# W_v in column quarters, five x buffers, a halved norm scaling, and a list scheduler that counts table loads, in an eight-core encoder block

## The chip, the cores and the metric

The kernel runs on the eight cores of one Trainium2 chip. Every core computes one of eight batch entries with the same program; the cores exchange nothing. The metric is device microseconds of the slowest core. A run on eight cores can be in a slower state: one die, or both, is granted a lower TensorE clock and the run takes some per cent longer. Stage times are medians over the eight cores of one profiled fast run. Ratios are the mean time of one kernel's fast runs over that of the other's fast runs of the same rounds, so they are not quite the ratio of the medians quoted. "The V stage ends" means the start of its last matmul; in the same way attention ends with its last product with V, the convolution with the first matmul on W_out, and the output projection with the last one.

## The reference, cut to what matters

```python
# x (8, 2048, 2048) f32; one layer
h = rms_norm(x, ln1_g)
u = h @ W_in                                # 2048 -> 5120: conv value, conv gate, q, k, v
y_conv = conv_mixer(c_val, c_gate, ...)     # GLU, causal depthwise conv (31), LayerNorm, swish
y_attn = chunked_relbias_attention(q, k, v) # 8 heads of 128, 64-frame chunks, 9-chunk band
y = concat(rms_norm(y_conv), rms_norm(y_attn))
x = x + y @ W_out
x = x + relu(rms_norm(x) @ W1)**2 @ W2      # 2048 -> 8192 -> 2048
```

On a core the program has five stages: norm and V projection ("V stage"), attention with the q and k projections, convolution, output projection (beside the convolution group's normalisation), and feed-forward.

## The kernel before

The program is a list of operations. When the kernel is built, a list scheduler places them with a simple cost model and thereby fixes the order on each engine; at run time each engine works through its list and waits on semaphores. An operation at the head of a list that has to wait therefore blocks everything behind it, ready or not. The dependencies come from a table of who last wrote or read each granule of 64 bytes in SBUF:

```python
XLAT = 180.0
DMA_LAT = 2000.0
DMA_BPNS = 310.0          # the scheduler's belief of the DMA rate, bytes per ns
...
    # Prog.keys: an access touches these granules of SBUF
    for g in range(a // 64, (e - 1) // 64 + 1):
        for q in range(p0 // 32, (p0 + np_ - 1) // 32 + 1):
            out.add(g * 4 + q)
...
    # Prog.schedule: the ready operation of lowest program number goes next
            o.start = c
            busy[e] = c + o.dur
            if o.dma:
                s = max(dma_free, busy[e])
                dma_free = s + o.bytes / DMA_BPNS     # one first-in-first-out pipe
                o.end = dma_free + DMA_LAT
...
                rt[s] = max(rt[s], o.end + lat)       # when a successor may start
```

The V stage. A tile of x is normalised into `hb`, transposed on TensorE, copied to `hT`, and multiplied by W_v into a bank of PSUM, the memory that matmuls write to. The eviction is the ScalarE operation that copies the result from the bank to V. V has a row of 8 heads x 130 elements for every tile of 128 tokens (two further columns of ones give the softmax sums):

```python
V = sb("V", [16, 8, 130], BF16, B)
wv = sb("wv", [2, 16, 512], BF16, C)                   # W_v in two column halves
xs1 = [sb(f"xa{i}", [2048], F32, D0 + 8192 * i) for i in range(3)]
...
loadx(0); pv; gr                                       # gr: the norm's gain row
for j in range(4):                                     # gain row to all partitions
    mm(ps(4 + j), <ones>, gr[0:1, j * 512:(j + 1) * 512], True, True)
    copy(g1[:, j * 512:(j + 1) * 512], ps(4 + j))      # VectorE
for q in range(4):                                     # first half, in quarters of its rows
    P.dma("pool", f"wv0{q}", wv[:, 0, 4 * q:4 * q + 4, :], ...)
late = [... second half, after tile 1 ...]

def norm_tile(xt, t, st, r, g, hbuf, dst, banks):
    act(hbuf[:, :], xt, AF.Square, accum=st[:, t, 0:1])
    act(st[:, t, 1:2], st[:, t, 0:1], AF.Ln, ...)
    act(r[:, t:t + 1], st[:, t, 1:2], AF.Exp, scale=-0.5)
    stt(hbuf[:, :], xt, r[:, t:t + 1], g, ALU.mult, ALU.mult)    # the scaling
    ... 16 transposes on TensorE, two copies to hT ...

for t in range(NT):
    norm_tile(...)
    for hf in range(2):
        b = nb[0] % 4                                  # four PSUM banks in turn
        nb[0] += 1
        for k in range(16):
            mm(ps(b), hT[...tile t, block k...], wv[:, hf, k, :], k == 0, k == 15)
        act(V[:, t, 4 * hf:4 * hf + 4, 0:128], ps(b)..., AF.Identity)   # the eviction
```

`norm_tile` also serves the second norm (tile h2b), inside the output projection stage.

## Time and profile before

Four timed runs took 2789.91, 2790.71, 2901.05 and 3006.79 us, the last two slow; the profiled run took 2791.73 us and is a fast one.

From the profile page of the kernel before (its slowest core): the span, TensorE's busy time, TensorE's busy tenths in 40 slices, and the granted clock in tenths.

```profile
span 2790.2 us, 37523 instructions; the slowest of 8 cores (2783.8 to 2790.2 us)
PE 2727.9 (98%) x14192; PEld 1271.9 (46%) x14192; DVE 930.0 (33%) x1460; ACT 822.6 (29%) x1561; POOL 227.9 (8%) x367
PE   6999999999989999999999999999999999999999
PEclk9999999999999999999999999999999999999999
```

TensorE is the bound, and 98% busy looks like nothing is left. But a busy TensorE need not be at its peak. Taking from the timeline the time from each matmul's start to the next one's, and subtracting its columns at 2.4 GHz, leaves about 117 us (core 3; 2654 us are the columns). Two places stand out: the first 60 us (23 us of it) and 700 to 1020 us (39 us). Another 34 us lie in small pieces between 100 and 700 us.

The windows view of core 3 before, in stretches of 100 us (stretch, its length, busy us and instruction count of TensorE, weight loads, VectorE, ScalarE, GpSimd; then the granted clock, DMA share and GB/s):

```profile
700.00:800.00 100.00, 88.36 (x640) 42.46 (x639) 82.79 (x110) 60.85 (x86) 22.73 (x22) 1.00 0.54 148
800.00:900.00 100.00, 90.18 (x532) 44.48 (x531) 66.75 (x93) 63.18 (x82) 1.79 (x2) 0.97 0.46 132
900.00:1000.00 100.00, 96.00 (x551) 47.91 (x550) 51.12 (x58) 38.84 (x54) 1.43 (x2) 0.98 0.47 143
1300.00:1400.00 100.00, 100.00 (x465) 45.37 (x464) 17.87 (x26) 19.66 (x32) 5.71 (x8) 1.00 0.46 75
```

The last line is the feed-forward part: 465 matmuls of 512 columns in 100 us, 215 ns each, with no gap. In the three lines above it TensorE sits idle part of the time. The waits view of core 3 before (who waited for whom: total us, times, longest) names the largest:

```profile
PE ps L158 <- DVE h2b L193: 13.8, 4, 4.1
PE ps L158 <- DVE hb_75 L193: 8.9, 3, 4.3
PE ps L158 <- DVE hb_76 L193: 5.1, 2, 3.4
```

h2b is the second norm's scaled tile, in the output projection; hb is the first norm's, in the V stage. The start is best read in the timeline of TensorE on core 3 before (start, length, operation, count, and in brackets the idle time before it and what ended that):

```profile
6.63 7.16 PE L154 MATMUL ps<-gr,onef 1*128 1x512 f32 x8 [6.63 <-DMA gr<-gvec]
17.37 1.86 PE L158 MATMUL ps<-identb,hb_75 128*128 128x128 bf16 x16 [3.58 <-DVE hb_75 L193]
19.44 1.86 PE L154 MATMUL ps<-wv,hT 128*128 128x512 bf16 x4 [0.20 <-DVE hT L184]
...
30.86 11.21 PE L154 MATMUL ps<-wv,hT 128*128 128x512 bf16 x40
...
50.30 7.99 PE L154 MATMUL ps<-wv,hT 128*128 128x512 bf16 x32
```

By 50 us only 48 V matmuls of 512 columns are done; from then on TensorE does not stop. The V stage ends at 161.5 us.

One more view matters, the ScalarE timeline before (core 5), in the output projection:

```profile
812.61 0.61 ACT L173 ACTIVATE jk_122<-sl_120 128x512 bf16<-128x512 f32 x1
813.23 1.28 ACT L173 ACT_TABLE_LOAD   x1
814.52 0.30 ACT L173 ACTIVATE st<-st,pv 128x1 f32<-128x1 f32 x1
```

A change between Silu and Ln or Exp costs a table load of 1.28 us. The profile has 25 of them, and the scheduler's model has none.

### The profile page before, as it was taken

What the parts mean: (1) busy time and instruction counts of PE and PEld (TensorE: products, weight loads), DVE (VectorE), ACT (ScalarE), POOL (GpSimd) and SP (SyncE); (2) the same over time, 40 slices, a digit from 0 to 9 for tenths busy, and PEclk for the clock granted to TensorE, in tenths of its full rate; (3) what the DMA queues carried; (4) which work ended last, traced back from release to release, by engine and by line L of the source; (5) the groups of instructions that cost most, each with busy time, mean ns of one, the idle gap of its engine ahead of it and who ended that gap; (6) DMA issues with size and microseconds to landing.
All of it is one profiled execution on the core that took longest, in us unless ns stands there. A gap on an engine that the chain in (4) does not pass through costs nothing.

```text
span 2790.2 us, 37523 instructions; the slowest of 8 cores (2783.8 to 2790.2 us)
## 1 busy us (share of the span) xinstructions
PE 2727.9 (98%) x14192; PEld 1271.9 (46%) x14192; DVE 930.0 (33%) x1460; ACT 822.6 (29%) x1561; POOL 227.9 (8%) x367
## 2 busy tenths in 40 slices
PE   6999999999989999999999999999999999999999
PEld 3545555444444444444444444444444444444444
DVE  3435556555876532021131120221311302203113
ACT  3437777211485331201202112112021021120220
POOL 0000000423300000000000000000000000000000
PEclk9999999999999999999999999999999999999999
DMA  8611110335644467444444444468644444444424
GB/s 197 153 33 35 35 28 2 61 55 88 146 137 136 136 151 183 79 76 78 80 76 77 78 76 76 76 137 195 136 76 76 76 76 76 77 77 76 78 41 136
DMA packets 112737, 256.77 MB, mean 92 GB/s; under 512 B 5425, under 2 KB 83249, under 8 KB 95153
## 3 DMA queue, kind: packets, MB, share of 16 engines
q0 software_dynamic: 92400, 167.82, 36.8%
q1 hardware_dynamic: 20162, 86.56, 8.9%
q8 instruction: 117, 1.92, 0.3%
q14 instruction: 58, 0.48, 0.1%
HBM read 388.60 MB, written 33.55 MB: 151 GB/s over the span
## 4 chain that ended last, share of the span: by engine, by line
PE 93%; DVE 2%; ACT 2%; issue 2%; DMA 1%; POOL 0%; SPq 0%; DVEq 0%; ACTq 0%; POOLq 0%
PE ps L154 91%; PE ps L158 1%; DMA xa_73<-x 1%; DVE Gt_110 L201 0%; DVE h2b L193 0%; DMA eB_94<-relb 0%; DVE Gt_109 L201 0%; DVE G L193 0%; ACT L173 0%; DVE y L193 0%; DVE y L201 0%; DVE hb_75 L193 0%; POOL pad L184 0%; ACT cs L173 0%; ACT hb_75 L173 0%
## 5 line engine op out<-in xcount | busy, mean ns | idle before, releaser
L187 DVE TENSOR_TENSOR acc<-acc,ps 128x512 f32<-128x512 f32 x512 | 351.7, 688 | 1412.3 <-PE ps L154 1408.5
L154 PE MATMUL ps<-yb,fT 128*128 128x512 bf16 x2752 | 598.8, 379 | 0.0
L154 PEld LDWEIGHTS ps<-yb,fT 128*128 128x128 bf16 x2752 | 269.0, 98 | 325.1 <-issue 1.6
L173 ACT ACTIVATE rl_131<-ps 128x512 f32<-128x512 f32 x128 | 76.6, 598 | 1101.1 <-PE ps L154 1098.5
L154 PE MATMUL ps<-w2s_135,fT 128*128 128x512 bf16 x1344 | 293.9, 379 | 0.0
L154 PE MATMUL ps<-hTb,yb 128*128 128x512 bf16 x1024 | 242.1, 379 | 0.0
L154 PE MATMUL ps<-yb 128*128 128x512 bf16 x1024 | 241.9, 379 | 0.0
L154 PEld LDWEIGHTS ps<-w2s_135,fT 128*128 128x128 bf16 x1344 | 131.5, 98 | 158.6 <-issue 0.3
L220 POOL DMA_DIRECT2D yb<-w x75 | 66.3, 883 | 1189.4 <-PE ps L154 1112.4
L173 ACT ACTIVATE rl_132<-ps 128x512 f32<-128x512 f32 x128 | 76.6, 598 | 270.8 <-PE ps L154 270.8
L154 PEld LDWEIGHTS ps<-yb 128*128 128x128 bf16 x1024 | 100.2, 98 | 120.8
L154 PEld LDWEIGHTS ps<-hTb,yb 128*128 128x128 bf16 x1024 | 100.1, 98 | 120.6
L154 PE MATMUL ps<-yb,w1s_133 128*128 128x512 bf16 x512 | 121.0, 379 | 0.0
L154 PE MATMUL ps<-hTb,w1s_134 128*128 128x512 bf16 x512 | 121.0, 379 | 0.0
L154 PE MATMUL ps<-yb,w1s_134 128*128 128x512 bf16 x512 | 121.0, 379 | 0.0
L154 PE MATMUL ps<-hTb,w1s_133 128*128 128x512 bf16 x512 | 120.9, 379 | 0.0
L154 PE MATMUL ps<-wo,yT 128*128 128x512 bf16 x512 | 119.0, 386 | 1.4 <-ACT yT L173 0.9
L154 PE MATMUL ps<-hT,wc_101 128*128 128x512 bf16 x512 | 119.6, 379 | 0.0
L154 PE MATMUL ps<-wo,yb 128*128 128x512 bf16 x512 | 118.5, 389 | 0.0
L154 PE MATMUL ps<-wv,hT 128*128 128x512 bf16 x512 | 116.5, 389 | 0.4 <-DVE hT L184 0.2
L154 PE MATMUL ps<-hT,wc_102 128*128 128x512 bf16 x512 | 116.1, 379 | 0.9 <-DMA wc_102<-wcg 0.9
L154 PE MATMUL ps<-hT,wqk_66 128*128 128x512 bf16 x384 | 97.1, 379 | 0.0
(269 smaller groups left out, 2688.8 us busy)
## 6 DMA issues: line engine op xcount, KB each, us to landing
yb<-w POOLq DMA_DIRECT2D x75, 1024.0 KB, 8.8
w2s_135<-w POOLq DMA_DIRECT2D x21, 1024.0 KB, 8.4
w1s_133<-w POOLq DMA_DIRECT2D x16, 1024.0 KB, 8.4
w1s_134<-w POOLq DMA_DIRECT2D x16, 1024.0 KB, 8.4
acc<-out SPq DMA_DIRECT2D x16, 1024.0 KB, 9.8
out<-acc SPq DMA_DIRECT2D x64, 256.0 KB, 5.8
wo<-wo POOLq DMA_DIRECT2D x8, 1024.0 KB, 13.7
xa_71<-x SPq DMA_DIRECT2D x6, 1024.0 KB, 6.7
```

What stands on the lines that cost most here:

```text
L154: self.op("pe", lambda e: e.matmul(out, lhsT=lhsT, rhs=rhs, start=start, stop=stop, skip_group_check=skip), [lhsT, rhs], [out], f * max(n ...
L158: self.op("pe", lambda e: e.transpose(out, in_, ident), [in_, ident], [out], 64.0)
L173: self.op("act", lambda e: e.activation(out=out, in_=in_, func=func, scale=scale, bias=bias, **kw), r, w, d)
L187: self._ew(eng, lambda e: e.tensor_tensor(out=out, in0=in0, in1=in1, op=op), [in0, in1], [out], fast)
L220: o = self.op(eng, lambda e: e.dma_start(out=out, in_=in_), r, w, 900.0 if eng == "pool" else 350.0, dma=True, key=key, nbytes=nb)
```

## The change

Its intent: feed TensorE earlier at the start, and give the scheduler a truer model, so that the fixed order blocks less. The diff cut to its core:

```diff
+SLACK = 400.0
+TABLE = 1300.0
+    SETS = ((AF.Exp, AF.Ln), (AF.Exp, AF.Tanh), (AF.Silu,))
             busy[e] = c + o.dur
+            if o.func in (AF.Exp, AF.Ln, AF.Tanh, AF.Silu) and o.func not in tset:
+                tset = next(s for s in self.SETS if o.func in s)
+                busy[e] += TABLE
...
+                if so.eng == "pe" and e != "pe":
+                    lat += SLACK          # TensorE may use another engine's result 400 ns later
...
-    wv = sb("wv", [2, 16, 512], BF16, C)
+    wv = sb("wv", [4, 16, 256], BF16, C)
-    xs1 = [... for i in range(3)]
+    xs1 = [... for i in range(5)]         # and hb from two buffers to three
-    loadx(0); pv; gr
+    gr; loadx(0); identity; pv            # the gain row first
-        copy(g1[...], ps(4 + j))
+        copy(...) if j % 2 else act(..., AF.Identity)
+    ld = []
+    for j in range(4):
+        ld.append(P.dma("pool", f"wv{j}", wv[:, j, :, :], wv_d[j]))
+        if j == 0:
+            for t in range(1, 5):
+                loadx(t)
...
-        stt(hbuf[:, :], xt, r[:, t:t + 1], g, ALU.mult, ALU.mult)
+        for hf in range(2):
+            c = slice(1024 * hf, 1024 * hf + 1024)
+            stt(hbuf[:, c], xt[:, c], r[:, t:t + 1], g[:, c], ALU.mult, ALU.mult)
...
+            if hf and t < 8: act(o_, src, AF.Identity)   # every other hT copy of the first 8 tiles
...
-        for hf in range(2):
-            b = nb[0] % 4
+        for hf in range(4):                              # bank = quarter
             for k in range(16):
-                mm(ps(b), hT[...], wv[:, hf, k, :], k == 0, k == 15)
-            act(V[:, t, 4 * hf:4 * hf + 4, 0:128], ...)
+                mm(ps(hf, 0, 256), hT[...], wv[:, hf, k, :], k == 0, k == 15)
+            act(V[:, t, 2 * hf:2 * hf + 2, 0:128], ...)
+    for j in (1, 2, 3):
+        ld[j].deps.add(xo_[2 * j - 1].i)                 # quarters 2, 3, 4 after x tiles 1, 3, 5
```

Smaller edits are cut: the modelled byte count of a DMA now uses its true number of partitions, and the hT copies are modelled as faster.

More of the change, by code (lines that the diff above doesn't have):

```diff
@@ L28 @@
 class Op:
-    __slots__ = ("i", "eng", "fn", "dur", "deps", "dma", "key", "cnt", "bytes", "prio",
+    __slots__ = ("i", "func", "eng", "fn", "dur", "deps", "dma", "key", "cnt", "bytes", "prio",
                  "start", "end", "pos", "signal", "waits", "ins")
@@ L44, in __init__ @@
         self.cnt = 0
+        self.func = None
 class Prog:
@@ L172, in act @@
             d += 100
-        self.op("act", lambda e: e.activation(out=out, in_=in_, func=func, scale=scale, bias=bias, **kw), r, w, d)
+        self.op("act", lambda e: e.activation(out=out, in_=in_, func=func, scale=scale, bias=bias, **kw), r, w, d).func = func
     def _ew(self, eng, fn, r, w, fast=1.0):
@@ L181, in _ew, with copy @@
         self.op(eng, fn, r, w, d)
-    def copy(self, out, in_, eng="dve"):
-        self._ew(eng, lambda e: e.tensor_copy(out=out, in_=in_), [in_], [out])
+    def copy(self, out, in_, eng="dve", fast=1.0):
+        self._ew(eng, lambda e: e.tensor_copy(out=out, in_=in_), [in_], [out], fast)
     def tt(self, out, in0, in1, op, eng="dve", fast=1.0):
@@ L218, in dma @@
                 l.append(x)
-                nb = max(nb, self.n(x) * 128 * 4)
+                nb = max(nb, self.n(x) * x.ap[0][1] * 4)
         o = self.op(eng, lambda e: e.dma_start(out=out, in_=in_), r, w, 900.0 if eng == "pool" else 350.0, dma=True, key=key, nbytes=nb)
@@ L240, in schedule @@
         dma_free = 0.0
+        tset = ()
         for o in ops:
@@ L394, in build_program @@
     x_d = dr("x", [S, D])
-    wv_d = dr("wv", [2, 128, 16, 512])
+    wv_d = dr("wv", [4, 128, 16, 256])
     wqk_d = dr("wqk", [8, 2, 128, 16, 128])
@@ L471, in build_program @@
     wqk = [sb(f"wqk{i}", [16, 128], BF16, o + 16384 + 4096 * i) for i in range(3)]
-    wv = sb("wv", [2, 16, 512], BF16, C)
+    wv = sb("wv", [4, 16, 256], BF16, C)
     on = sb("on", [16, 1024], BF16, C)
-    xs1 = [sb(f"xa{i}", [2048], F32, D0 + 8192 * i) for i in range(3)]
+    xs1 = [sb(f"xa{i}", [2048], F32, (D0, D0 + 8192, D0 + 16384, B + 33280, B + 41472)[i]) for i in range(5)]
     g1 = sb("g1", [2048], F32, D0 + 24 * KB)
-    hb = [sb(f"hb{i}", [2048], BF16, D0 + 32 * KB + 4096 * i) for i in range(2)]
+    hb = [sb(f"hb{i}", [2048], BF16, (D0 + 32 * KB, D0 + 36 * KB, B + 57856)[i]) for i in range(3)]
+    xo_ = {}
     def loadx(t):
-        P.dma("sp", f"xa{t % 3}", xs1[t % 3][:, :], x_d[t * 128:(t + 1) * 128, :])
+        xo_[t] = P.dma("sp", f"xa{t % 5}", xs1[t % 5][:, :], x_d[t * 128:(t + 1) * 128, :])
     def bcast(g, n):
         return bass.AP(gv_d.tensor, g * 2048, [[0, 128], [1, n]])
-    loadx(0)
-    P.dma("sp", "pv", pv[:, :], pv_d)
     gr = sb("gr", [2048], F32, D0 + 42 * KB)
     P.dma("sp", "gr", gr[0:1, :], gv_d[0:1, :])
+    loadx(0)
+    P.dma("pool", "id", identb[:, :], id_d)
+    P.dma("sp", "pv", pv[:, :], pv_d)
     P.memset(onef[:, :], 1.0, "dve")
@@ L491, in build_program @@
         mm(ps(4 + j), bass.AP(onef, 0, [[1, 1], [0, 128]]), gr[0:1, j * 512:(j + 1) * 512], True, True)
-        copy(g1[:, j * 512:(j + 1) * 512], ps(4 + j))
-    P.dma("pool", "id", identb[:, :], id_d)
-    P.dma("sp", "sel", sel[:, :], id_d[:, 0:4])
-    for q in range(4):
-        P.dma("pool", f"wv0{q}", wv[:, 0, 4 * q:4 * q + 4, :], wv_d[0][:, 4 * q:4 * q + 4, :])
-    late = [P.dma("pool", f"wv1{q}", wv[:, 1, 8 * q:8 * q + 8, :], wv_d[1][:, 8 * q:8 * q + 8, :]) for q in range(2)]
-    loadx(1)
-    loadx(2)
+        if j % 2:
+            copy(g1[:, j * 512:(j + 1) * 512], ps(4 + j))
+        else:
+            act(g1[:, j * 512:(j + 1) * 512], ps(4 + j), AF.Identity)
+    ld = []
[4 more added lines that the diff above has]
+                loadx(t)
+            P.dma("sp", "sel", sel[:, :], id_d[:, 0:4])
     P.ts(pv[:, bdw2:bdw2 + 8], pv[:, bdw:bdw + 8], 2.0, ALU.mult)
@@ L506, in build_program @@
     P.memset(V[:, :, :, 128:130], 1.0, "pool")
-    nb = [0]
     def norm_tile(xt, t, st, r, g, hbuf, dst, banks):
-        act(hbuf[:, :], xt, AF.Square, accum=st[:, t, 0:1])
+        act(hbuf[:, :], xt[:, :], AF.Square, accum=st[:, t, 0:1])
         act(st[:, t, 1:2], st[:, t, 0:1], AF.Ln, scale=1.0 / D, bias=pc(epsc))
         act(r[:, t:t + 1], st[:, t, 1:2], AF.Exp, scale=-0.5)
-        stt(hbuf[:, :], xt, r[:, t:t + 1], g, ALU.mult, ALU.mult)
+        for hf in range(2):
+            c = slice(1024 * hf, 1024 * hf + 1024)
+            stt(hbuf[:, c], xt[:, c], r[:, t:t + 1], g[:, c], ALU.mult, ALU.mult)
         for hf in range(2):
@@ L527, in dst @@
             o_ = hT[:, qd, 8 * hf:8 * hf + 8, ti * 128:(ti + 1) * 128]
-            copy(o_, src)
-        norm_tile(xs1[t % 3][:, :], t, st, rn, g1[:, :], hb[t % 2], dst, (4 + 2 * (t % 2), 5 + 2 * (t % 2)))
-        if t + 3 < NT:
-            loadx(t + 3)
-        if t == 1:
-            for o_ in late:
-                o_.deps.add(len(P.ops) - 1)
+            if hf and t < 8:
+                act(o_, src, AF.Identity)
+            else:
+                copy(o_, src, fast=1.9)
+        norm_tile(xs1[t % 5], t, st, rn, g1, hb[t % 3], dst, (4 + 2 * (t % 2), 5 + 2 * (t % 2)))
+        if t + 5 < NT:
+            loadx(t + 5)
         if t == 8:
             mark = len(P.ops) - 1
-        for hf in range(2):
-            b = nb[0] % 4
-            nb[0] += 1
+        for hf in range(4):
             for k in range(16):
-                mm(ps(b), hT[:, qd, k, ti * 128:(ti + 1) * 128], wv[:, hf, k, :], k == 0, k == 15)
-            act(V[:, t, 4 * hf:4 * hf + 4, 0:128], ps(b).rearrange("p (h c) -> p h c", c=128), AF.Identity)
+                mm(ps(hf, 0, 256), hT[:, qd, k, ti * 128:(ti + 1) * 128], wv[:, hf, k, :], k == 0, k == 15)
+            act(V[:, t, 2 * hf:2 * hf + 2, 0:128], ps(hf, 0, 256).rearrange("p (h c) -> p h c", c=128), AF.Identity)
+    for j in (1, 2, 3):
+        ld[j].deps.add(xo_[2 * j - 1].i)
     q32 = [sb(f"q32{i}", [512], F32, D0 + 40 * KB + 2048 * i) for i in range(2)]
@@ L800, in out_conv @@
         P.dma("sp", f"xw{t % 3}", out_d[t * 128:(t + 1) * 128, :], xs[t % 3][:, :], w=[("x1", t)])
-        norm_tile(xs[t % 3][:, :], t, st, rn, g2[:, :], h2b, dst, (3, 4))
+        norm_tile(xs[t % 3], t, st, rn, g2, h2b, dst, (3, 4))
     conv_load(0)
@@ L965, in _prep_shared @@
     wvv = win[:, 4096:5120]
-    wv = np.stack([kc(wvv[:, i * 512:(i + 1) * 512], 512) for i in range(2)])
+    wv = np.stack([kc(wvv[:, i * 256:(i + 1) * 256], 256) for i in range(4)])
     wcg = np.stack([np.stack([kc(win[:, o + i * 128:o + (i + 1) * 128], 128) for o in (0, 1024)], 1) for i in range(8)])
```

## The prediction

> All numbers are of the fast state (profiled run 2791.73 us; the timed runs of 2901 and 3007 us are read as slow ones). A slow run would lie some per cent above.
>
> **What bounds it now.** TensorE: 98% busy on the page, 91% of the chain of waits. Charging every matmul of the timeline its columns at 2.4 GHz gives about 2654 us; start-to-start time beyond that is about 121 us, plus 8.0 us before the first matmul. From 1020 us on (feed-forward) the windows view shows 465 matmuls per 100 us, 215 ns each: the change can't touch it. The excess lies in three places: 0 to 60 us, about 30 us with the 8 us before the first matmul; 100 to 700 us (attention, convolution), about 34 us in small pieces; 700 to 1000 us (output projection beside the convolution group's normalisation), about 40 us.
>
> **The start.** Before, the gain row lands at 7.96 us, its broadcast takes 7.16 us, four VectorE copies end at 15.9, the scaling takes 2.35, and the first transpose starts at 18.70. Four matmuls on W_v run at 20.8; the rest of its first half waits until 32.9 us (timeline); the second half, issued at 35.2, comes around 50. By 50.9 us TensorE has done about 15 us of work. DMA is 90 to 100% busy until 60 us, so only order helps. After: the gain row lands near 4 us, the copies alternate with ScalarE, the scaling comes in halves (about 1.2 us each): first transpose near 13 us. Four x tiles and one column quarter at a time give complete accumulations earlier: estimated 30 us of useful work by 50 us. Saved: 16 us (8 to 22). Added: V is 1024 matmuls of 256 columns instead of 512 of 512, about 3 ns more each (2 us), and 32 more evictions on ScalarE, 40 to 50% busy there.
>
> **The scheduler.** The trace has 25 table loads of 1283 ns, 21 of them in 700 to 1000 us, which the old cost model counted as nothing. The Trainium skill ("ScalarE: Activation LUTs", What ACT_TABLE_LOAD costs) gives about 1283 ns plus a drain; the trace agrees on the load. The static TensorE order therefore reaches transposes too early: four waits for h2b, 13.9 us in all (waits view). Such waits also drop the clock: the windows view shows 0.95 to 0.98 in 700 to 1000 us, about 10 us; the skill ("TensorE: Matmul & The Clock Gate", What's actually happening) describes this half rate after idling, and this trace has such stretches of 3.4 us. I expect the table cost, the 400 ns slack and the first scaling half to take away 18 us here (8 to 26), and the slack about 6 us (0 to 12) in 100 to 700 us. Table loads themselves: still 20 to 30.
>
> **Sum.** 2791.7 - 16 - 18 - 6 = about 2752 us, -1.4%. Range 2725 to 2785. Over 2% needs 56 us of roughly 130 removable at most: 0.2. Slower by 2%: 0.02. Within 2%: 0.78.
>
> **What would show it.** First transpose at 12 to 14 us; end of the V stage (162.8 us before) at 143 to 152; waits for h2b below 5 us; clock in 700 to 900 us above 0.98; feed-forward still 215 ns per matmul, starting about 40 us earlier.
>
> **What would make it wrong.** The x tiles sharing DMA with the first column quarter so that it lands after 25 us, and later quarters waiting behind x: the start gains little. A static order that puts V of a late quarter ahead of transposes and blocks. Slack pulling filler work forward, so that the stage from 700 us lacks it. New stalls in the feed-forward part. And a gain near 50 us if the waits of 700 to 1000 us vanish wholly.

## The result, and the profile after

Four fast runs took 2782.34 to 2785.23 us, median 2783.81. The fast runs' ratio to those of the kernel before is 0.9977, 95% interval 0.9953 to 1.0001: the same, where 0.986 was forecast. From the profile page after (the profiler lost some matmul records of this core):

```profile
span 2782.1 us, 38484 instructions; the slowest of 8 cores (2778.2 to 2782.1 us)
PE 2707.2 (97%) x14445; PEld 1327.1 (48%) x14704; DVE 932.3 (34%) x1482; ACT 830.9 (30%) x1601; POOL 228.1 (8%) x365
PE   4999999999989999999999999999999999999999
PEclk8999999999999999999999999999999999999999
```

The first slice fell from 6 to 4 tenths, and its clock from 9 to 8: the start got worse. The other end of the argument went as forecast. The windows view of core 3 after:

```profile
700.00:800.00 100.00, 89.61 (x676) 43.26 (x673) 76.97 (x100) 53.53 (x76) 30.84 (x29) 0.95 0.57 142
800.00:900.00 100.00, 97.74 (x575) 47.85 (x576) 79.12 (x115) 67.26 (x91) 2.00 (x2) 0.97 0.49 148
900.00:1000.00 100.00, 100.00 (x600) 50.22 (x599) 56.31 (x69) 43.07 (x56) 1.92 (x3) 1.00 0.47 148
1300.00:1400.00 100.00, 100.00 (x465) 45.31 (x463) 17.73 (x27) 19.62 (x32) 5.18 (x7) 1.00 0.47 79
```

TensorE is busy for 97.74 and 100 us where it was for 90.18 and 96, and the feed-forward line is unchanged. The waits of core 3 after: those for hb doubled, from 14.0 to 28.4 us, and h2b almost went.

```profile
PE ps L163 <- DVE hb_77 L198: 11.5, 5, 4.1
PE ps L163 <- DVE hb_78 L198: 9.7, 6, 3.4
PE ps L163 <- DVE hb_79 L198: 7.2, 1, 7.2
...
PE ps L163 <- DVE h2b L198: 1.1, 2, 0.6
```

The start on TensorE, core 3 after:

```profile
2.92 7.16 PE L159 MATMUL ps<-gr,onef 1*128 1x512 f32 x8 [2.92 <-DMA gr<-gvec]
14.15 2.10 PE L163 MATMUL ps<-identb,hb_77 128*128 128x128 bf16 x16 [4.07 <-DVE hb_77 L198]
21.10 3.57 PE L159 MATMUL ps<-wv,hT 128*128 128x256 bf16 x16 [4.84 <-DMA wv<-wv]
...
29.22 1.91 PE L159 MATMUL ps<-wv,hT 128*128 128x256 bf16 x8
...
31.57 1.07 PE L159 MATMUL ps<-wv,hT 128*128 128x256 bf16 x8
...
41.09 1.01 PE L163 MATMUL ps<-identb,hb_78 128*128 128x128 bf16 x8 [3.35 <-DVE hb_78 L198]
...
50.52 1.01 PE L163 MATMUL ps<-identb,hb_79 128*128 128x128 bf16 x8 [7.22 <-DVE hb_79 L198]
51.33 3.62 PE L159 MATMUL ps<-wv,hT 128*128 128x256 bf16 x16
```

The transposes do start earlier (17.4 to 14.2 us). The first weight quarter is there at 21.0. But between 32.6 and 51.3 us there is no V matmul at all, only transposes waiting for later x tiles; by 50.5 us 32 V matmuls of 256 columns are done, a third of the work that was done before. In that stretch the data are there: the trace has the second quarter landing at 38.0 us, the third at 46.7, and four tiles normalised by 37. The line at 50.52 names one reason: TensorE waits 7.22 us for the sixth x tile, which landed at 45.5, and the first tile's second quarter stands behind that tile's transposes in the list. ScalarE's timeline after (core 3) shows the other side. These are its evictions of V, with one Square between them:

```profile
24.82 0.39 ACT L178 ACTIVATE V<-ps 128x256 bf16<-128x256 f32 x1 [1.96 <-PE ps L159]
...
45.54 1.91 ACT L178 ACTIVATE hb_79<-xa_71 128x2048 bf16<-128x2048 f32 x1 [5.99 <-DMA xa_71<-x]
...
55.04 0.38 ACT L178 ACTIVATE V<-ps 128x256 bf16<-128x256 f32 x1 [5.14 <-PE ps L159]
...
66.25 0.39 ACT L178 ACTIVATE V<-ps 128x256 bf16<-128x256 f32 x1 [2.13 <-PE ps L159]
...
76.46 1.34 ACT L178 ACTIVATE V<-ps 128x256 bf16<-128x256 f32 x3 [2.16 <-PE ps L159]
```

The second tile's first quarter was multiplied by 32.6 us. Yet until 76 us ScalarE evicts only three pieces of V, and then they come in bursts. Something makes the second tile's eviction wait for the fourth piece, the first tile's last quarter, whose weights land at 60.8 us.

The granted clock falls too. The windows view of core 3, 40 to 60 us, before and then after:

```profile
40.00:60.00 20.00, 15.50 (x95) 8.73 (x94) 10.70 (x9) 6.67 (x13) 0.00 (x0) 0.83 0.94 229
40.00:60.00 20.00, 8.98 (x64) 7.03 (x64) 6.49 (x7) 8.01 (x12) 0.53 (x1) 0.61 1.00 282
```

At the lower clock the work costs more: the 16 matmuls at 51.33 us take 3.62 us, 226 ns each, where a later row of 400 takes 109.6 ns each (core 0). In the first 100 us TensorE is idle for 21.5 us before and 35.7 after (medians of the cores), 14 us more; counting half of its busy time at half clock as lost, the clock took an estimated 3.7 us before and 7.2 after. So of the 20 us lost below about 14 are idle time and an estimated 3 to 4 are clock.

The stages, medians over the eight cores, in us (each stage from the end of the one before; the span's median is 2786 before and 2780 after):

| stage | before | after | difference | predicted |
|---|---|---|---|---|
| V stage ends at | 161.5 | 181.6 | +20.1 | -16 |
| attention | 324.6 | 320.8 | -3.8 | -6 with the next |
| convolution | 236.9 | 228.1 | -8.8 | |
| output projection | 286.7 | 273.5 | -13.2 | -18 |

So the scheduler's gain came (25.8 us against 24 predicted), and the start gave 20 us of it back instead of adding 16.

### The profile page after: what moved, and what is told of

It is laid out like the page before. It is cut to its first block, busy times and chain, and to the rows that moved or that the text cites. A ratio compares the mean times of both kernels' runs of the same rounds, so it can differ in the third digit from the quotient of the medians.

```text
span 2782.1 us, 38484 instructions; the slowest of 8 cores (2778.2 to 2782.1 us)
## 1 busy us (share of the span) xinstructions
PE 2707.2 (97%) x14445; PEld 1327.1 (48%) x14704; DVE 932.3 (34%) x1482; ACT 830.9 (30%) x1601; POOL 228.1 (8%) x365
## 3 DMA queue, kind: packets, MB, share of 16 engines
q0 software_dynamic: 92112, 167.82, 37.9%
## 4 chain that ended last, share of the span: by engine, by line
PE 94%; DMA 2%; issue 2%; DVE 1%; ACT 1%; ACTq 0%; DVEq 0%; SPq 0%; POOLq 0%
PE ps L159 93%; DMA xa_71<-x 1%; PE ps L163 1%; DMA acc<-out 1%; DMA wc_105<-wcg 0%; DVE y L198 0%; DVE y L192 0%; DVE hb_77 L198 0%; DVE Gt_113 L206 0%; ACT L178 0%; ACT hb_77 L178 0%; DVE hb_78 L198 0%; DVE y L206 0%; DVE yb L203 0%; DVE h2b L198 0%
## 5 line engine op out<-in xcount | busy, mean ns | idle before, releaser
L159 PE MATMUL ps<-wv,hT 128*128 128x256 bf16 x1024 | 120.6, 281 | 5.4 <-DMA wv<-wv 4.0
L159 PE MATMUL ps<-hT,wc_105 128*128 128x512 bf16 x498 | 115.0, 381 | 3.4 <-DMA wc_105<-wcg 2.5
L159 PE MATMUL ps<-hT,wc_104 128*128 128x512 bf16 x496 | 117.4, 379 | 0.9
L159 PEld LDWEIGHTS ps<-wv,hT 128*128 128x128 bf16 x1024 | 102.6, 101 | 20.6 <-issue 6.3
```

The lines of the kernel that those rows point to most:

```text
L159: self.op("pe", lambda e: e.matmul(out, lhsT=lhsT, rhs=rhs, start=start, stop=stop, skip_group_check=skip), [lhsT, rhs], [out], f * max(n ...
```

## The experiments

The main theory (G) came from the code. A row of V for one tile is 8 x 130 x 2 = 2080 bytes, which is 32.5 granules of 64. The last bytes of tile 0 and the first of tile 1 share a granule, so the dependency table makes tile 1's first quarter wait for tile 0's last quarter, though they write different bytes. A quarter's 520 bytes end inside a granule as well, so the eight evictions of tiles 0 and 1 form one chain; tile 2 starts on a fresh granule (4160 bytes are 65). With halves in four rotating banks that costs little. With the quarter bound to its bank, tile 1's first quarter keeps bank 0, and no later tile can use bank 0 until the last weight quarter has come. Rivals: the transfers are simply too late (D); 256-column matmuls cost more (N); the scheduler's belief of the DMA rate is too high (S); the scheduler's new terms made the start slow. Intervals exist for e1, e2, e4, e6 and e8 only; e12 has two fast runs and the others one each, so these are read by their stage times. Within one undisturbed profile the end of the V stage differs by up to 7 us between the cores, so differences of 1 or 2 us between medians decide nothing.

### e1: V stored head by head

```diff
-    V = sb("V", [16, 8, 130], BF16, B)
+    V = sb("V", [8, 16, 130], BF16, B)
-    act(V[:, t, 2 * hf:2 * hf + 2, 0:128], ...)
+    act(V[:, 2 * hf:2 * hf + 2, t, 0:128], ...)
```

> The changed kernel with one edit: V is stored head by head instead of tile by tile, so that the evictions of one tile's first quarter and the tile before's last quarter no longer touch the same 64-byte granule of the dependency bookkeeping. No transfer, duration or size changes. Theory G (false dependency: the second tile's first quarter can't be evicted before the first tile's last quarter, which needs the last weight quarter at about 60 us): the V stage ends at 152 to 168 us instead of 182, the waits for hb in the first 75 us fall from about 28 to under 12 us, the whole time falls by 15 to 30 us to 2754 to 2769. Rival D (the x tiles and weight quarters simply land too late): V still ends within 4 us of 182 and the time stays at 2780 to 2787. Rival N (256-column matmuls cost more): likewise no change.

V ends at 166.4 us instead of 181.6 and the time is 2769.47 us (ratio to before 0.9894, 0.9842 to 0.9947), just above the range expected. A head's row of 16 tiles is 4160 bytes, 65 whole granules, so quarters no longer share any. The first three weight quarters land within 1.2 us of those in the change and the last one later (62.0 against 60.8 us, core 3), so D and N can't explain these 15 us; G is shown. The scheduler builds its order anew in e1, so the 15 us are the false dependency together with the order that it forced. The evictions of V on ScalarE (core 3 of e1) now come as their matmuls end:

```profile
24.90 0.38 ACT L178 ACTIVATE V<-ps 128x256 bf16<-128x256 f32 x1 [1.90 <-PE ps L159]
...
33.38 0.39 ACT L178 ACTIVATE V<-ps 128x256 bf16<-128x256 f32 x1 [0.87 <-PE ps L163]
...
39.94 0.36 ACT L178 ACTIVATE V<-ps 128x256 bf16<-128x256 f32 x1
```

But V still ends 5 us later than before, so this is not all.

### e2: the same layout in the kernel before

> The kernel before with the same layout edit. Theory G says that halves in four rotating banks hide most of the false dependency, since two tiles can be in flight: V ends 0 to 6 us earlier than 162.6, time 2783 to 2790. If the layout itself had another effect (reading V in the second attention product), the attention stage from 163 to 489 us would change by more than 2 us here.

V ends at 162.2 us, attention takes 324.1, and the ratio is 0.9997 (0.9908 to 1.0086). No effect of the layout by itself is seen, and the false dependency was harmless in the kernel before: it needed the change's quarters and fixed banks to bite.

### e3: the kernel before with the scheduler's part alone

> The kernel before with the scheduler's part of the change alone (table loads counted, 400 ns slack before TensorE), start untouched. If attention to output projection gains come from the scheduler: span from V's end to the end of the output projection falls by 20 to 30 us from 852 us and waits for h2b from 13.9 to under 4 us; the time is 2760 to 2772 provided V still ends near 162. If instead the gains came from the halved scaling, the output projection keeps its waits and the time stays above 2780.

One run was undisturbed: 2764.01 us. In the profiled run two cores had a lower clock (0.984 and 0.986, at 2786 and 2789 us); the other six took 2755 to 2761, and so did the undisturbed die of a slow run (2756 to 2760). From V's end to the last output projection matmul it is 820.5 us against 848.3: the scheduler's part alone is worth about 28 us, and beats the whole change by 20.

### e4: the change with table cost and slack set to zero

> The changed kernel with table cost and slack set to zero. If the scheduler's part only helps after the V stage: V still ends at 178 to 186 us, the later gain of about 27 us is mostly lost, and the time is 2800 to 2812, slower than before. If the scheduler's part made the start slow, V ends below 170 us and the time is at most 2795.

V ends at 185.8 us and the three fast runs are at 2815.4 to 2816.2, 3 to 4 us beyond the expected range (the ratio to before is 1.006, 0.9991 to 1.0129, so not clearly slower). The slow start is not the scheduler's new terms. The output projection takes 288.0 us here although its scaling is halved: the halves alone mend nothing there.

### e5: e1 with a lower belief of the DMA rate

```diff
-DMA_BPNS = 310.0
+DMA_BPNS = 235.0
```

> The changed kernel with V head by head (as e1), and the scheduler's belief of the DMA rate lowered from 310 to 235 bytes per ns; only the static order changes. In e1 the sixth x tile lands at about 45 us where the scheduler assumed about 30, and TensorE and ScalarE sit in their fixed order behind it (a wait of 5.7 us for hT on one core). Theory S (what is left of the slow start is that optimism): V ends 5 us or more earlier than the 163 to 168 us of e1. Rival D (transfers simply land too late): V ends within 3 us of e1. Orders after V may change too; only the V stage is read here.

V ends at 166.9 us, as in e1, and the output projection is 6 us longer. This one number does not mend the order. S falls in this form.

### e6: e1 with three x buffers

```diff
-    xs1 = [... for i in range(5)]      # t % 5, t + 5
+    xs1 = [... for i in range(3)]      # t % 3, t + 3
```

> As e1, but with three x buffers as before the change instead of five. Theory S and D together: five buffers put four x tiles into competition with the first weight quarter; with two, the first quarter lands 3 to 5 us earlier than 21 us, but the fourth x tile later. Net: V ends within 4 us of e1's 163 to 168, so the five buffers are worth nothing either way; time 2762 to 2772. If the deep prefetch is what helps the start, V ends over 5 us later than in e1.

V ends at 157.1 us, 9.3 earlier, and the time is 2759.98 us (ratio to before 0.9893, 0.9873 to 0.9912). The expectation missed in two ways: it allowed no such gain, and the first quarter lands no earlier (21.2 us against 21.1 on core 3). Five buffers hurt, and not by way of the first quarter.

### e7: the change, weights not waiting for x tiles

```diff
-    for j in (1, 2, 3):
-        ld[j].deps.add(xo_[2 * j - 1].i)
```

> The changed kernel with V tile by tile (false dependency kept), but the weight quarters 2 to 4 no longer wait for x tiles to land. Theory G: the whole pipeline hangs on the first tile's LAST quarter, so bringing it in at about 40 to 45 us instead of 60 ends V 8 to 15 us earlier than 182 us, though x tiles get later. If G were wrong and the x tiles were the limit, slower x tiles would make V end at 182 us or later.

V ends at 173.0 us, 8.6 earlier. The last quarter now lands at 48.6 us (core 3). With the false dependency kept, bringing it in sooner helps, as G says, although the x tiles land later (the fourth at 39.2 us instead of 27.3).

### e8: before, with the scheduler's part, the gain row first and halves

This is e3 with the layout of e2, the gain row's transfer first, its copies shared with ScalarE, the scaling in halves and the true byte count of a DMA. W_v stays in halves, x has three buffers.

> The kernel before with the scheduler's part, V head by head, the gain row first, its copies shared with ScalarE and the scaling in halves; W_v still in halves and three x buffers. First transpose at 13 to 15 us as in the change. If the first 5 us of the start reach the end: V ends at 155 to 159 us and the time is 2757 to 2761, against about 2764 for the scheduler's part alone. If the start is bound by the transfers of W_v (first half complete at 33 us), the 5 us are lost again: V ends at 160 to 164 and the time is 2761 to 2766.

V ends at 155.0 us, and the fast runs are at 2756.0 to 2758.7 us: 0.9885 of before (0.9865 to 0.9904), and 26 us better than the change. This is the best kernel with an interval.

### e9 and e10: table cost alone, slack alone

Both are e3 with the other constant set to zero.

> The kernel before with the table-load cost in the scheduler alone (no slack). Whole scheduler part (e3): from V's end to the last output projection matmul 820.5 us against 848.3 before, of which attention 319.5 against 324.6, convolution 228.1 against 236.9, output projection 272.5 against 286.7 (medians of the cores). If the table cost is what mends the output projection stage, that stage falls to 272 to 278 here while attention and convolution keep 323 to 325 and 235 to 238. If the slack does it, all three keep the values of before within 2 us.

> The kernel before with the 400 ns slack alone. The counterpart of e9: attention should fall to 318 to 321 and convolution to 227 to 230, where no or few tables are loaded; the output projection keeps 280 to 288 if the table cost is the cure there, and falls to 271 to 276 if the slack is.

| us | before | table only (e9) | slack only (e10) | both (e3) |
|---|---|---|---|---|
| attention | 324.6 | 325.5 | 318.5 | 319.5 |
| convolution | 236.9 | 234.3 | 233.5 | 228.1 |
| output projection | 286.7 | 274.6 | 290.0 | 272.5 |
| waits for h2b (slowest core) | 13.9 | 2.1 | 14.9 | 2.0 |

The table cost mends the output projection, where the table loads are; the slack mends attention. In the convolution each gives about 3 us and both together 9, more than their sum; why was not tested, and e10's expectation for it (227 to 230) missed. Two other expectations missed slightly: e9's convolution (235 to 238) and e10's output projection (280 to 288). The number of table loads did not fall (27 on the profiled core of e3, 25 before): knowing their cost moved the work around them, it did not save them.

### e11: e8 with the scaling in one piece

> As e8, but the norm's scaling in one piece again. e8's first transpose is at 13.3 us and its V stage ends at 155.0 (core median) against 162.2 and 163.2 without the gain row first and without halves. If the gain row alone does that: first transpose near 14.6, V ends within 1.5 us of 155. If the halves matter on every tile of the start: V ends 3 us or more later.

The first transpose is at 14.6 us and V ends at 161.6, 6.6 later than in e8. So the gain row first is worth 1 us or less at the end of the stage (161.6 against 162.2 in e2, inside the spread of the cores), and the halves nearly all the rest, although they bring the first transpose forward by only 1.3 us. Each of the first tiles waits through the same chain, so the saving can recur; that it recurs in just this way was not shown, because the static order differs too, and the granted clock as well (0.74 and 0.83 in 20 to 40 and 40 to 60 us on core 3 of e11, 1.00 in both in e8; by the reckoning above an estimated 2 of the 6.6 us).

### e12: e6 with weights not waiting for x tiles

> As e6 (quarters, V head by head, three x buffers), but the weight quarters do not wait for x tiles. V ended at 157.1 in e6 with the last quarter landing at 57 us, and at 155.0 in e8 with halves. If earlier weights help, V ends at 150 to 155 and the time is 2753 to 2758, level with or better than e8's 2757. If the x tiles are then starved, V ends over 158.

V ends at 161.3 us, later than in e6 although the last quarter lands at 47.3 us; the two fast runs are at 2764.8 and 2765.2. Without the false dependency, holding the weights back behind x tiles is better: the fourth x tile lands at 47.1 us on core 3, against 28.4 in e6. The order was built anew here, so the run does not separate it from the transfers.

### e13 and e14: order against transfers

What do five buffers do? Either early x loads slow the weights, or the order made for early x loads blocks. In e13 the order is e1's and the x loads are delayed to e6's times; in e14 the order is e6's and the x loads run as early as in e1. The dependencies are changed between scheduling and emission, and the x tiles land as intended (the fifth, core 3: 42.8 us in e13 and 42.0 in e6; 38.5 in e14 and 37.9 in e1). Rebuilt from the kernels, e13's order equals e1's, and e14's equals e6's except at eight places of ScalarE's list near 120 us:

```diff
         self.schedule()
+        for a, b in self.swap:             # (x load t, scaling of tile t-3)
+            self.ops[a].deps.add(b)        # e13; e14: scheduled with it, then discard(b)
         self.sync()
```

> e1's static order on TensorE, ScalarE, VectorE, GpSimd and the queues, unchanged, but x tile t is loaded only after tile t-3 is scaled, as three buffers force in e6. Contention theory: V ends at 155 to 160 us, as e6 (157.1). Order theory: V ends at 164 to 170 us, as e1 (166.4) or later.

> e6's static order (the compute order is compared and equal), but with five x buffers, so that x tiles load as early as in e1. Contention theory: V ends at 164 to 170 us, as e1 (166.4). Order theory: V ends at 154 to 160 us, as e6 (157.1).

| V stage ends, us; in brackets the start of its 513th matmul of 1024 | x loads late | x loads early |
|---|---|---|
| order made for three buffers | 157.1 [94.3] (e6) | 155.5 [92.7] (e14) |
| order made for five buffers | 178.4 [103.0] (e13) | 166.4 [103.6] (e1) |

It is the order. Halfway through the stage the order is worth 9 to 11 us, and early or late loads less than 2 us, which is within the spread of the cores. The 12 us between e13 and e1 come later, most of them in one stall of 9 to 13 us on every core of e13 (timelines of ScalarE and TensorE, core 3):

```profile
134.34 0.42 ACT L179 ACTIVATE eB<-eB 128x256 f32<-128x256 f32 x1 [12.40 <-DMA eB<-relb]
139.21 8.92 PE L160 MATMUL ps<-wv,hT 128*128 128x256 bf16 x64 [10.86 <-DVE hT L190]
```

ScalarE's next operation in its list needs a load for the attention (relb), which was issued at 117.7 us as in e1 (118.8) but landed at 134.3 instead of 121.5. Why it took so long was not tested. Up to the 513th matmul e13 is level with e1, so 178.4 says nothing about late x loads at the start. The waits of core 3 in the first 100 us, of e13 and then of e14, name what stands in the way there:

```profile
PE ps L160 <- ACT V L179: 8.1, 2, 7.8
PE ps L164 <- DVE hb L199: 7.4, 6, 3.2
```

```profile
PE ps L164 <- DVE hb L199: 7.0, 4, 3.2
PE ps L160 <- DMA wv<-wv: 5.4, 1, 5.4
```

TensorE waits for ScalarE's evictions in e13 and not in e14. In e1 the same thing can be watched (timeline of core 3, all engines):

```profile
46.88 1.91 ACT L178 ACTIVATE hb<-xa 128x2048 bf16<-128x2048 f32 x1 [6.05 <-DMA xa<-x]
...
48.79 1.00 ACT L178 ACTIVATE hT<-ps 128x1024 bf16<-128x1024 bf16 x1
...
49.94 1.87 PE L159 MATMUL ps<-wv,hT 128*128 128x256 bf16 x8 [5.68 <-ACT hT L178]
```

The Square of the sixth x tile stands in ScalarE's list ahead of an hT copy. The tile lands 6 us after ScalarE is free; the copy, whose transposes had ended at 38.7, waits behind it, and TensorE waits for the copy.

## Why the prediction was right or wrong

- **What bounds the kernel, and where the excess lies.** Right. Feed-forward stayed at 215 ns per matmul.
- **The scheduler, "18 us here" and "about 6 us" in 100 to 700 us.** The sum was right (24 forecast, 25.8 measured), partly by luck: the output projection gave 13.2 us, less than forecast, and attention and convolution 12.6, twice as much. The waits for h2b fell below 5 us as forecast (1.1), and table loads stayed at 23. The clock did not rise above 0.98 in 700 to 900 us (0.95 and 0.97 on core 3). Of the three causes named together, e9 and e10 show that the table cost did it, and e4 that the halves alone did not.
- **The first transpose "near 13 us".** Right: 13.5.
- **The step that failed: "Four x tiles and one column quarter at a time give complete accumulations earlier: estimated 30 us of useful work by 50 us. Saved: 16 us (8 to 22)".** Measured: V ended 20.1 us later. The estimate multiplied tiles that had arrived by quarters that had arrived, as if any such pair could run. Two fixed things forbade it. First, tile 1's eviction had to wait for tile 0's last quarter, through shared 64-byte granules (15.2 us, e1). Second, the order built for five buffers put ScalarE's work on x tiles that had not landed ahead of work that was ready (9.3 us between e1 and e6; e13 and e14 show it is the order). Even with both cured the saving is 4.4 us (e6) to 6.0 us (e14), not 16, so the estimate was too large besides; why was not traced. Quarters with both cured (157.1) were no better than halves (155.0).
- **"What would make it wrong".** The first quarter was on time (21 us, not after 25). A static order that blocks was named, but the wrong one: not late quarters ahead of transposes, but transposes of later tiles ahead of V, because the order had V wait for its bank. New stalls in feed-forward did not come.
- **256-column matmuls.** The fear was small and so is the cost. In the timeline after (core 0) 400 of them in a row took 43.83 us, 109.6 ns each, which agrees with an estimate from the Trainium skill, 256 / 2.4 + 2.5 = 109.2 ns ("TensorE: Matmul & The Clock Gate", Wait — 56ns, not 53.3ns?).

What stays open: why the scheduler's order for five buffers is so poor. Lowering its DMA rate to 235 bytes per ns did not mend it (e5). It models one first-in-first-out pipe, while the trace shows x tiles and weights from two queues side by side; a two-queue model was not tried.

## What to carry to other kernels

Before counting on "this piece and that piece have arrived, so the product can run", walk the chain of one piece's buffer: who must free the bank, and what that operation waits for, false dependencies of the bookkeeping included; splitting work finer multiplies the boundaries at which pieces share a granule. With a fixed order on each engine, a deeper prefetch is also a promise that the order is built on, and when a tile comes late everything behind it waits; so test the order and the transfers apart, as e13 and e14 do. And when a change has several parts, run each alone: the scheduler's two constants were worth about 28 us, and the start that came with them took most of that back.

## What the Trainium skill lacked or had wrong

- "ScalarE: Activation LUTs", What ACT_TABLE_LOAD costs: the page gives about 1283 ns for the load and a drain of about 1380 ns more, 2.66 us per switch. The load is confirmed (1283 ns in every profile read). The drain is not seen here: in the ScalarE timeline before, an activation ends at 813.22 us, the load starts at 813.23 and the next activation at 814.52, so the switch costs 1.3 us.
- "DMA: Bandwidth & Descriptors", Queues, rings and completion order: the page says that an engine takes turns between queues packet by packet, but not what share two queues get. From 8 to 21 us on core 3 after the change, the DMA view gives 2.04 MB written for the x queue and 1.02 MB for the weights' queue, which reads float32 and writes bf16, so 2.04 MB read: equal shares of the bytes read. From 21.3 to 38 us it gives 2.21 and 1.74 MB (3.48 read), so this is no fixed share.
